# The experts of a routed mixture on one Trainium2 core: the last product of one expert set behind the first two of the next, and a spectrum computed in pieces between

## The chip, the cores and the metric

The kernel runs on one core of a Trainium2 chip. The metric is the device time of one launch in microseconds (us), the median of the runs; less is better. The engines named below are PE (matrix products), DVE (VectorE, elementwise), ACT (ScalarE), POOL (GpSimd, here indirect gathers and scatters) and SP (issues the large loads). Each runs its own instructions in a fixed order, and they wait for each other through semaphores.

## The reference, cut to what matters

Two transformer blocks run in a row. The first ends in a mixture of 32 experts, of which each of the 1024 tokens goes to two. The reference, cut to the part of an expert:

```python
def run(args):                                   # one block of tokens of one expert
    xblk, e = args
    hid = jax.nn.silu(xblk @ w1[e]) * (xblk @ w3[e])   # 1024 -> 512, twice
    return hid @ w2[e]                                 # 512 -> 1024

yb = lax.map(run, (xb, blk_expert)).reshape(cap, D) * buf_w[:, None]
y = jnp.zeros((N, D)).at[buf_tok].add(yb)        # back to the tokens
```

The second block needs, long before its first product, the spectrum of a filter: for each of 1024 channels an implicit filter (a small product times a decaying window), its absolute sum, and its transform by tables of cosines and sines. It depends on nothing that the experts compute, so the kernel works it out while the experts run.

## The kernel before

**The experts.** The kernel sorts the tokens to 32 experts and gives them places: place 0 to 11 are "large" (one slot of 128 tokens; places 1 to 3 have a second slot of 64 tokens), places 12 to 31 are "small" (64 tokens each; two small ones share one gather of 128 rows). They run as: place 0, then eleven large ones, and behind each of the first ten of these a pair of small ones. Ten times, therefore, the program goes through a group of three: large, small, small.

**One expert** is `block(w, slots)` (L1442). Its weights come in six pieces of 1 MB: four of `w1` and `w3`, two of `w2`. `weights` (L217) handles each piece: SP loads it into one of five `raw` tiles (L223), ACT rounds it to a high part `hi` (L228), DVE takes the difference `lo` (L230); there are three pairs of `hi` and `lo` tiles, and a pair is free again when PE has used it. The products are three matmuls per tile in this split arithmetic (L235 to L237), or two where 64 tokens' high and low parts stand side by side (L1459, L1460). Then

- `h` (two PSUM banks, tag `mm`; the second slot's have tag `acc`) holds x·w1 and x·w3. ACT and DVE make silu(h1)·h3 in the tile `hs` (L1465, L1466; for 64 tokens L1470 to L1473, where the halves are added first);
- PE transposes `hs` into PSUM (L1476), ACT and DVE split it into `sh` and `sl` (L1479, L1480);
- PE multiplies by `w2` into two banks of tag `acc` (with two slots, the first slot's into `mm`); DVE scales the result into `yo` (L1496), and POOL adds it to the tokens by an indirect DMA (L1497).

All of this is written expert by expert. Tokens come by `gather` (L1423): an indirect DMA into one of three `xg` tiles (L1428), PE transposes (L1435), and a split by ACT and DVE into `x` (two tiles, L1438, L1439).

**The spectrum** is a generator (L291) that is drained in one go behind the last of the 32 experts (L1534). It has PSUM banks of its own (`sp`, two) and one tile of most kinds; so the output tile `so` (L368, L369) is one tile, and two SP transfers of 256 KB each (L371) must have written it to DRAM before it can be filled again.

**What sets the order.** The program is not run in the order in which it is written: a scheduler takes the written order as a priority and lays each engine's instructions in a list at build time, moving later work into gaps that it expects. So pieces of the spectrum stand between the experts' matmuls in the kernel before, too, and a few matmuls of the next expert stand ahead of the transposes of one. The list of each engine is then fixed.

Of the kernel before, what the change touches and what calls it, by code (L numbers as in the profile page):

```python
# [15 lines left out]
P = 128  # L16
# [5 lines left out]
NTWO = 3  # L22
NLARGE = 12

C1 = NLARGE
# [93 lines left out]
class Builder:  # L119
# [171 lines left out]
    def spectrum(self, fp):  # L291
# [17 lines left out]
        for b in range(2):  # L309
# [14 lines left out]
            for q in range(8):  # L324
# [17 lines left out]
                if q == 0:  # L342
                    nc.vector.tensor_tensor(asum, ab, sd[q][1], op=ALU.max)
                else:
                    nc.vector.tensor_tensor(ab, ab, sd[q][1], op=ALU.max)
                    nc.gpsimd.tensor_tensor(asum, asum, ab, op=ALU.add)
            t = self.sp()
# [3 lines left out]
            for u in range(2):  # L351
                for mm in range(2):
# [9 lines left out]
                    nc.vector.tensor_add(ev[0], ev[0], q[1])  # L362
                    for n in range(2):
# [6 lines left out]
                        for v in range(2):  # L370
                            nc.sync.dma_start(spec[4 * b:4 * b + 4, :, 2 * u + v, mm + 2 * n, :].rearrange("c p n -> p c n"),  # L371
                                              o[:, v, :].rearrange("p (c n) -> p c n", n=P))

# [1033 lines left out]
    def moe(self):  # L1407
        nc, tc, I = self.nc, self.tc, self.i
        h2 = self.scr["h2"]
        with ExitStack() as cx:  # L1410
# [31 lines left out]
            def block(w, slots, eng=None):  # L1442
# [18 lines left out]
                hs = []  # L1461
                for n, (rows, x, tcol, gcol) in zip(N, slots):
# [4 lines left out]
                    else:  # L1467
# [5 lines left out]
                        nc.vector.tensor_mul(s[0:64], s[0:64], v[0:64])  # L1473
                    t = self.tp((P, 4, rows))
# [6 lines left out]
                    hs.append((sh, sl))  # L1481
# [23 lines left out]
            def place(b):  # L1505
                return of(nc.sync.value_load(self.order[0:1, b - 1:b], min_val=0, max_val=31))

            def large(b):
# [7 lines left out]
                return slots  # L1516

            def small(c):

                x = gather(self.tokI[:, c:c + 1], P, True)  # L1520
                for e, (t, g) in enumerate(((self.tokI[0:64, c:c + 1], self.gateS[0:64, c:c + 1]),
                                            (self.tokB[:, c - C1:c - C1 + 1], self.gateB[:, c - C1:c - C1 + 1]))):
                    block(place(NLARGE + 2 * (c - C1) + e), [(64, x[:, :, e], t, g)])

            block(lambda nm: I[nm][0, 0], large(0), nc.gpsimd)

            rest = list(range(NTWO + 1, NLARGE))
            for n, at in enumerate((2, 5, 8)):
                rest.insert(at, n + 1)
            for n, b in enumerate(rest):  # L1530
                block(place(b), large(b))
                if n < C2 - C1:
                    small(C1 + n)
# [5 lines left out]
            with tc.For_i(0, count, 1) as it:  # L1539
# [5 lines left out]
                block(of(reg), [(P, gather(tk), tk, gk)])  # L1545
# [390 lines left out]
```

## Time and profile before

| | |
|---|---|
| median of 3 runs | 3360.79 us (3357.3 to 3363.08) |
| the profiled execution | 3357.9 us, span 3356.1 us |
| busy share of the span | PE 92%, DVE 73%, ACT 39%, POOL 7% |
| experts, 1282 to 2075 us of the span | 793 us: PE busy 685.83, DVE 606.55, ACT 464.48 us |
| in that stretch | granted clock 0.93 of full, DMA share 0.81, 281 GB/s |

The span is that of one execution taken by the profiler; what lies around it (1.8 us) is the same for both kernels. Busy PE is a union of matmuls that overlap in their pipeline. [...] The DMA share is the mean busy share of the core's 16 DMA engines.

### The profile page before, as it was taken

The page shows a single profiled execution, that of the slowest core. Times are in us where ns is not written, and L with a number is a line of the kernel's source. Part 1 is how long each engine was busy: PE and PEld are TensorE (multiplying, and loading weights), DVE is VectorE, ACT ScalarE, POOL GpSimd, SP SyncE. Part 2 cuts the span into 40 slices and gives each one's busy share as a digit, 9 for nine tenths or more (in the row PEclk, how much of TensorE's full clock was granted, in tenths as well). Part 3 has the DMA queues.
Part 4 walks back from the last instruction along what each step waited for, and adds up shares of the span by engine and source line. Part 5 has one row for each costly group of instructions (what it writes and reads, how often), then busy time and mean ns, then how long its engine had stood idle before and what let it go on. Part 6 is the DMA issues. An engine that isn't in the chain of part 4 may idle for free. (4 is left out here: it accounts for less than half of the span.)

```text
span 3356.1 us, 41235 instructions
## 1 busy us (share of the span) xinstructions
PE 3077.4 (92%) x15219; PEld 2438.3 (73%) x15219; DVE 2438.7 (73%) x4447; ACT 1305.6 (39%) x1990; POOL 237.0 (7%) x143
## 2 busy tenths in 40 slices
PE   5999999999999959897899876899999999999998
PEld 4789999877777826565566554688887788888886
DVE  7888878667676577878778665577778765755767
ACT  3443333455543225657656554422233221221222
POOL 0000000000000012312213111000000000000000
PEclk9999999999999959998899988899999999999999
DMA  5653424244247346988789875322124311111111
GB/s 189 197 185 117 125 73 130 76 141 131 87 143 267 132 149 241 325 260 289 259 291 314 292 244 178 137 76 76 63 76 170 113 51 50 51 51 48 47 38 69
DMA packets 287912, 499.16 MB, mean 149 GB/s; under 512 B 21482, under 2 KB 176278, under 8 KB 286685
## 3 DMA queue, kind: packets, MB, share of 16 engines
q1 hardware_dynamic: 272925, 465.03, 40.8%
q0 software_dynamic: 6976, 16.79, 2.1%
q10 hardware_dynamic: 7808, 14.68, 1.2%
q8 instruction: 121, 1.98, 0.2%
q14 instruction: 82, 0.67, 0.1%
HBM read 431.92 MB, written 72.38 MB: 150 GB/s over the span
## 5 line engine op out<-in xcount | busy, mean ns | idle before, releaser
L230 DVE TENSOR_TENSOR lo<-raw,hi 128x2048 fp32r<-128x2048 f32 (+1 forms) x274 | 531.7, 1957 | 220.0 <-ACT hi L228 216.7
L228 ACT CAST hi<-raw 128x2048 fp32r<-128x2048 f32 (+1 forms) x276 | 449.6, 1644 | 270.3 <-PE acc L237 144.5
L243 PE MATMUL mm<-y_lo,hi 128*128 128x512 f32 x1072 | 423.1, 395 | 0.0
L244 PE MATMUL mm<-y_hi,lo 128*128 128x512 f32 x1072 | 423.0, 395 | 0.0
L246 PE MATMUL mm<-y_hi,hi 128*128 128x512 f32 x1072 | 273.6, 395 | 0.0
L243 PEld LDWEIGHTS mm<-y_lo,hi 128*128 128x128 f32 x1072 | 201.7, 188 | 44.9 <-DVE y_lo L215 0.2
L244 PEld LDWEIGHTS mm<-y_hi,lo 128*128 128x128 f32 x1072 | 201.7, 188 | 44.6
L246 PEld LDWEIGHTS mm<-y_hi,hi 128*128 128x128 f32 x1072 | 200.9, 188 | 44.5
L1852 DVE SCALAR_TENSOR_TENSOR cv<-gpad,fcw,cv 128x1024 f32<-128x1024 f32 x176 | 225.9, 1283 | 5.1
L243 PE MATMUL mm<-h_lo,hi 128*128 128x512 f32 x448 | 179.2, 401 | 0.5 <-DVE h_lo L215 0.5
L244 PE MATMUL mm<-h_hi,lo 128*128 128x512 f32 x448 | 178.0, 398 | 0.0
L416 DVE SCALAR_TENSOR_TENSOR ada<-araw,c,ada 128x512 f32<-128x512 f32 (+1 forms) x176 | 139.9, 795 | 30.9 <-DMA araw<-in_mod_w 15.8
L1459 PE MATMUL mm<-lo,x 128*128 128x512 f32 x320 | 137.5, 430 | 26.7 <-DVE lo L230 22.3
L243 PE MATMUL mm<-lo,h_hi 128*128 128x256 f32 x512 | 135.8, 296 | 0.1
L244 PE MATMUL mm<-hi,h_lo 128*128 128x256 f32 x512 | 133.3, 291 | 0.0
L1460 PE MATMUL mm<-hi,x 128*128 128x512 f32 x320 | 128.0, 400 | 0.0
L246 PE MATMUL mm<-h_hi,hi 128*128 128x512 f32 x448 | 121.8, 398 | 0.0
L1497 POOL DMA_INDIRECT d_x<-yo,tokI x25 | 96.5, 3859 | 345.4 <-DVE yo L1496 311.5
L235 PE MATMUL acc<-hi,sh 128*64 128x512 f32 (+1 forms) x256 | 117.2, 458 | 3.5 <-ACT sh L1479 3.5
L236 PE MATMUL acc<-lo,sh 128*64 128x512 f32 (+1 forms) x256 | 111.4, 435 | 0.0
L1796 ACT CAST hi<-raw 128x2048 fp32r<-128x2048 f32 (+2 forms) x36 | 63.6, 1767 | 122.7 <-PE tp L246 115.9
L1848 DVE TENSOR_SCALAR cv<-gpad,fcw,fcb 128x1024 f32<-128x1024 f32 x22 | 17.9, 814 | 121.7 <-ACT gpad L1842 121.6
(621 smaller groups left out, 6947.7 us busy)
## 6 DMA issues: line engine op xcount, KB each, us to landing
raw<-in_w SPq DMA_DIRECT2D x192, 1024.0 KB
araw<-in_mod_w SPq DMA_DIRECT2D x96, 256.0 KB
raw<-in_w_in SPq DMA_DIRECT2D x22, 1024.0 KB
raw<-in_ffn_w_up SPq DMA_DIRECT2D x44, 512.0 KB
araw<-in_w_ada SPq DMA_DIRECT2D x64, 256.0 KB
raw<-in_hy_w_in SPq DMA_DIRECT2D x12, 1024.0 KB
araw<-in_w_ada SPq DMA_DIRECT2D x16, 512.0 KB
d_G<-cy ACTq DMA_DIRECT2D x16, 512.0 KB
```

Source lines behind the costliest of these rows:

```text
L228: nc.scalar.copy(fh[:, qs], fr[:, qs])
L230: (eng or nc.vector).tensor_tensor(fl[:, qs], fr[:, qs], fh[:, qs].bitcast(F32), op=ALU.subtract)
L235: nc.tensor.matmul(out, lhs[0], rhs[0], start=start, stop=False)
L236: nc.tensor.matmul(out, lhs[0], rhs[1], start=False, stop=False)
L243: nc.tensor.matmul(out, a[0], b[1], start=start and k == 0, stop=False)
L244: nc.tensor.matmul(out, a[1], b[0], start=False, stop=False)
L246: nc.tensor.matmul(out, a[0], b[0], start=False, stop=stop and k == n - 1)
L416: V.scalar_tensor_tensor(acc, raw, c[:, k:k + 1], acc, op0=ALU.mult, op1=ALU.add)
L1459: nc.tensor.matmul(h[n][u], xx, wt[1][:, k, :], start=kk == 0, stop=False)
L1460: nc.tensor.matmul(h[n][u], xx, wt[0][:, k, :], start=False, stop=kk == 7)
L1497: nc.gpsimd.indirect_dma_start(out=self.x1, out_offset=bass.IndirectOffsetOnAxis(ap=tcol, axis=0), in_=yo[0:rows], in_offset=None, bounds_ ...
L1852: nc.vector.scalar_tensor_tensor(c3, g[:, di:di + 16, dj:dj + 64], col(k), c3, op0=ALU.mult, op1=ALU.add)
```

## The change

`block` is cut into three: `hidden` (products by w1 and w3, and `hs`), `turned` (transposes of `hs`, `sh` and `sl`) and `result` (product by w2 and the scatter). A loop takes the experts from a generator, one ahead: the gather of an expert is written ahead of the expert before it; then `hidden` of this expert, `result` of the one before it, `turned` of this one. The weights are loaded in the same changed order (four pieces of one expert, then the two pieces of w2 of the one before). The spectrum gets more `yield`s (40 pieces behind the loads at its start), and two pieces are written behind each of the 20 small experts. No product, no byte and no tile is added or removed.

```diff
@@ spectrum @@
                     nc.gpsimd.tensor_tensor(asum, asum, ab, op=ALU.add)
+                yield
...
                     nc.vector.tensor_add(ev[0], ev[0], q[1])
+                    yield
...
                             nc.sync.dma_start(spec[4 * b:4 * b + 4, :, 2 * u + v, mm + 2 * n, :].rearrange("c p n -> p c n"),
                                               o[:, v, :].rearrange("p (c n) -> p c n", n=P))
+                        yield
@@ moe @@
-            def block(w, slots, eng=None):
+            def hidden(w, slots, eng=None):
...
-                hs = []
+                out = []
...
+                    out.append(s)
+                return out
+
+            def turned(slots, hs):
+
+                out = []
+                for (rows, x, tcol, gcol), s in zip(slots, hs):
                     t = self.tp((P, 4, rows))
...
-                    hs.append((sh, sl))
+                    out.append((sh, sl))
+                return out
+
+            def result(w, slots, hs):
+
+                N = range(len(slots))
...
-            block(lambda nm: I[nm][0, 0], large(0), nc.gpsimd)
-
-            rest = list(range(NTWO + 1, NLARGE))
-            for n, at in enumerate((2, 5, 8)):
-                rest.insert(at, n + 1)
-            for n, b in enumerate(rest):
-                block(place(b), large(b))
-                if n < C2 - C1:
-                    small(C1 + n)
...
+            def experts():
+
+                yield from large(0)
+                rest = list(range(NTWO + 1, NLARGE))
+                for n, at in enumerate((2, 5, 8)):
+                    rest.insert(at, n + 1)
+                for n, b in enumerate(rest):
+                    yield from large(b)
+                    if n < C2 - C1:
+                        yield from small(C1 + n)
+
+
+            todo, before = experts(), None
+            nxt = next(todo)
+            while nxt:
+                (b, slots), nxt = nxt, next(todo, None)
+                w = place(b)
+                hs = hidden(w, slots, None if b else nc.gpsimd)
+                if before:
+                    result(*before)
+                before = w, slots, turned(slots, hs)
+
+                for _ in range(2 if b >= NLARGE else 0):
+                    next(spectrum, None)
+            result(*before)
             for _ in spectrum:
                 pass
```

Three places of the engines' lists show what this does. Line numbers of the kernel after are larger by 3 in `gather` and `hidden`, by 10 in `turned`, by 11 to 15 in `result`.

**PE at the end of a small expert.** Before, the four transposes of `hs` stand behind the last hidden matmuls (`mm<-..,x`) of the same expert, with one matmul of the spectrum (`sp`) between, and the w2 products (`acc<-..,sh`) behind them:

```order
L1459 MATMUL mm<-lo,x 128x512
L1460 MATMUL mm<-hi,x 128x512
L366 MATMUL sp<-sd_17807,dftl 128x512
L1476 MATMUL tp<-ident,hs 128x64 x4
L1435 MATMUL tp<-ident,xg_12745 128x128 x3
L235 MATMUL acc<-hi,sh 64x512
L236 MATMUL acc<-lo,sh 64x512
```

After, in the same place, the transposes stand behind the 24 w2 products of the expert before, and hidden matmuls of the next expert follow:

```order
L235 MATMUL acc<-hi,sh 128x512
L236 MATMUL acc<-lo,sh 128x512
L237 MATMUL acc<-hi,sl 128x512
L1486 MATMUL tp<-ident,hs 128x64 x4
L368 MATMUL sp<-sd_13872,dftl 128x512
L368 MATMUL sp<-sd_13887,dftl 128x512
L1438 MATMUL tp<-ident,xg_12744 128x128 x4
L1462 MATMUL mm<-lo,x 128x512
L1463 MATMUL mm<-hi,x 128x512
```

Between the matmuls that fill `h` and the transposes of `hs` there now stand 24 matmuls that need neither.

**DVE near the end of the spectrum.** `so` (L370, L371 after the change) is one tile, and `lo` is the splitting of a weight piece. After, two fillings of `so` stand this close:

```order
L370 TENSOR_TENSOR so<-ev,sp 128x512
L371 TENSOR_TENSOR so<-sp,ev 128x512
L230 TENSOR_TENSOR lo<-raw,hi 128x2048 x2
L370 TENSOR_TENSOR so<-ev,sp 128x512
L371 TENSOR_TENSOR so<-sp,ev 128x512
L230 TENSOR_TENSOR lo<-raw,hi 128x2048 x2
L1469 TENSOR_TENSOR hs<-hs,mm 128x512
```

In the kernel before, one of the closest two fillings has this between them, on the same engine:

```order
L368 TENSOR_TENSOR so<-ev,sp 128x512
L1439 TENSOR_TENSOR x<-tp,x 128x8x64 x2
L230 TENSOR_TENSOR lo<-raw,hi 128x2048
L369 TENSOR_TENSOR so<-sp,ev 128x512
L230 TENSOR_TENSOR lo<-raw,hi 128x2048
L1471 TENSOR_TENSOR hs<-mm,hs 64x512
L230 TENSOR_TENSOR lo<-raw,hi 128x2048
L368 TENSOR_TENSOR so<-ev,sp 128x512
```

There, two pieces of `lo` and a short instruction lie between a filling's end and the next one's start. Of the sixteen fillings three have come closer to the one before them than any is before: with two pieces of `lo` between (the one shown), with two and a scaled result, and with one piece and five short instructions. The spectrum also ends later: before, a third of the experts' rows in PE's list stand behind its last matmul; after, under a twentieth.

**PE and DVE at an expert with two slots** (three of the 32). After, PE's products by w2 of the expert before stand right behind the hidden matmuls of the second slot, and both write banks of tag `acc`:

```order
L1462 MATMUL acc<-lo,x 128x512
L1463 MATMUL acc<-hi,x 128x512
L235 MATMUL acc<-hi,sh 64x512
L236 MATMUL acc<-lo,sh 64x512
L237 MATMUL acc<-hi,sl 64x512
```

So they wait until DVE has read these banks out; on DVE the second of those two reads (`hs<-acc`, L1474) now stands here:

```order
L1474 TENSOR_TENSOR hs<-acc,hs 64x512
L230 TENSOR_TENSOR lo<-raw,hi 128x2048
L1442 TENSOR_TENSOR x<-tp,x 128x8x64 x2
L1469 TENSOR_TENSOR hs<-hs,mm 128x512
L1474 TENSOR_TENSOR hs<-acc,hs 64x512
```

One piece of `lo`, two splits of `x` and a product have come to stand between the two reads.

## Rows read from the trace of the kernel before

**Rows 1.** The page: engines' busy time, and slices of the span.

```profile
PE 3077.4 (92%) x15219; PEld 2438.3 (73%) x15219; DVE 2438.7 (73%) x4447; ACT 1305.6 (39%) x1990; POOL 237.0 (7%) x143
...
PEclk9999999999999959998899988899999999999999
...
GB/s 189 197 185 117 125 73 130 76 141 131 87 143 267 132 149 241 325 260 289 259 291 314 292 244 178 137 76 76 63 76 170 113 51 50 51 51 48 47 38 69
```

**Rows 2.** Stretches: start:end, length; busy PE, PEld, DVE, ACT, POOL; PEclk, DMA share, GB/s.

```profile
0.00:1199.00 1199.00, 1113.32 (x6754) 943.98 (x6754) 885.99 (x2575) 484.54 (x1080) 37.68 (x62) 0.99 0.44 142
1282.00:2075.00 793.00, 685.83 (x2666) 461.41 (x2664) 606.55 (x501) 464.48 (x389) 168.46 (x62) 0.93 0.81 281
2092.00:3356.10 1264.10, 1219.32 (x5655) 1001.87 (x5655) 874.93 (x1204) 334.38 (x496) 2.18 (x2) 0.98 0.23 75
```

**Rows 3.** The same view over three of the ten groups: the first two and the last.

```profile
1305.90:1376.80 70.90, 65.89 (x252) 42.78 (x252) 57.18 (x47) 41.46 (x34) 18.35 (x5) 0.95 0.91 320
1376.80:1453.30 76.50, 67.39 (x266) 45.94 (x265) 57.44 (x49) 42.19 (x37) 15.41 (x7) 0.93 0.94 319
...
1997.00:2070.00 73.00, 56.27 (x213) 39.78 (x213) 51.83 (x39) 40.72 (x32) 10.60 (x3) 0.86 0.68 241
```

**Rows 4.** Waits, 1282 to 2075 us: who waited for whom, us, times, longest.

```profile
DVE lo L230 <- ACT hi L228: 167.6, 54, 6.1
ACT hi L228 <- PE acc L237: 144.5, 55, 6.3
PE tp L1476 <- DVE hs L1473: 56.6, 15, 6.6
PE mm L1459 <- DVE lo L230: 22.3, 15, 5.9
DVE hs L1471 <- ACT hs L1470: 5.5, 11, 1.1
PE tp L1476 <- DVE hs L1466: 4.2, 3, 2.6
```

**Rows 5.** Timeline of a small expert: start, us, instruction, idle before and releaser.

```profile
2026.45 0.66 PE L1476 MATMUL tp<-ident,hs 64*128 64x64 f32 x4 [4.43 <-DVE hs L1473]
2027.57 0.69 PE L235 MATMUL acc<-hi,sh 128*64 128x512 f32 x1 [0.46 <-ACT sh L1479]
...
2032.32 0.47 PE L237 MATMUL acc<-hi,sl 128*64 128x512 f32 x1
2032.63 0.39 PE L235 MATMUL acc<-hi,sh 128*64 128x512 f32 x1
2032.86 0.39 PE L236 MATMUL acc<-lo,sh 128*64 128x512 f32 x1
...
2040.67 0.50 PE L1459 MATMUL mm<-lo,x 128*128 128x512 f32 x1 [1.38 <-DVE lo L230]
...
2044.61 0.40 PE L1460 MATMUL mm<-hi,x 128*128 128x512 f32 x1
...
2049.28 0.52 PE L1476 MATMUL tp<-ident,hs 64*128 64x64 f32 x4 [4.28 <-DVE hs L1473]
```

**Rows 6.** Groups by line, 1282 to 2075 us: count, busy us, mean ns, idle before.

```profile
L230 DVE TENSOR_TENSOR lo<-raw,hi 128x2048 fp32r<-128x2048 f32 x188 | 425.3, 2283 | 168.1 <-ACT hi L228 167.6
L228 ACT CAST hi<-raw 128x2048 fp32r<-128x2048 f32 x187 | 354.3, 1906 | 211.7 <-PE acc L237 144.5 <-issue 26.9 <-PE acc L1460 16.2
...
L1439 DVE TENSOR_TENSOR x<-tp,x 128x512 fp32r<-128x512 f32 (+1 forms) x48 | 30.1, 645 | 1.7 <-ACT x L1438 1.7
...
L1471 DVE TENSOR_TENSOR hs<-mm,hs 64x512 f32<-64x512 f32 x40 | 27.1, 678 | 3.1 <-ACT hs L1470 2.4
L1476 PE MATMUL tp<-ident,hs 64*128 64x64 f32 (+1 forms) x136 | 20.4, 284 | 60.8 <-DVE hs L1473 56.6 <-DVE hs L1466 4.2
```

**Rows 7.** Timeline of DVE: two fillings of so, neither preceded by a wait.

```profile
1481.20 0.68 DVE L369 TENSOR_TENSOR so<-sp,ev 128x512 f32<-128x512 f32 x1
...
1489.38 0.68 DVE L368 TENSOR_TENSOR so<-ev,sp 128x512 f32<-128x512 f32 x1
```

More of the change, by code (lines that the diff above doesn't have):

```diff
@@ L1505, in place @@
             def place(b):
-                return of(nc.sync.value_load(self.order[0:1, b - 1:b], min_val=0, max_val=31))
+                return of(nc.sync.value_load(self.order[0:1, b - 1:b], min_val=0, max_val=31)) if b else lambda nm: I[nm][0, 0]
             def large(b):
@@ L1515, in large @@
                     slots.append((64, gather(t, 64, True)[:, :, 0], t, g))
-                return slots
+                yield b, slots
             def small(c):
                 x = gather(self.tokI[:, c:c + 1], P, True)
-                for e, (t, g) in enumerate(((self.tokI[0:64, c:c + 1], self.gateS[0:64, c:c + 1]),
-                                            (self.tokB[:, c - C1:c - C1 + 1], self.gateB[:, c - C1:c - C1 + 1]))):
-                    block(place(NLARGE + 2 * (c - C1) + e), [(64, x[:, :, e], t, g)])
-            block(lambda nm: I[nm][0, 0], large(0), nc.gpsimd)
-            rest = list(range(NTWO + 1, NLARGE))
-            for n, at in enumerate((2, 5, 8)):
-                rest.insert(at, n + 1)
-            for n, b in enumerate(rest):
-                block(place(b), large(b))
-                if n < C2 - C1:
-                    small(C1 + n)
+                yield NLARGE + 2 * (c - C1), [(64, x[:, :, 0], self.tokI[0:64, c:c + 1], self.gateS[0:64, c:c + 1])]
+                yield NLARGE + 2 * (c - C1) + 1, [(64, x[:, :, 1], self.tokB[:, c - C1:c - C1 + 1], self.gateB[:, c - C1:c - C1 + 1])]
+            def experts():
[19 more added lines that the diff above has]
+            result(*before)
             for _ in spectrum:
@@ L1544, in moe @@
                 reg = nc.sync.value_load(self.eob[0:1, bass.ds(it, 1)], min_val=0, max_val=31)
-                block(of(reg), [(P, gather(tk), tk, gk)])
+                w, slots = of(reg), [(P, gather(tk), tk, gk)]
+                result(w, slots, turned(slots, hidden(w, slots)))
         self.psum(mm=4, acc=2, tp=2, aux=0)
```

## The prediction

> **What bounds the kernel now.** Read the page first: PE is busy 92% of the span, but the granted clock falls under 0.9 in a short dip (slice 14, counted from 0) and again in slices 18, 19 and 23 to 25, and in slices 16 to 23 the transfer rate is highest [rows 1]. That piece, slices 15 to 24, is the experts. Cut the span into stretches [rows 2]: ahead of the experts and behind them PE is busy 93% and 96% of the time at a clock of 0.99 and 0.98. In the 793 us of the experts PE is busy 685.83 us at 0.93, DVE 606.55 us, and the DMA engines 0.81 of the time. Nothing is full there, so something takes turns.
>
> The waits say what [rows 4]. Of the 107 us in which PE idles (793 - 686), 60.8 are spent in front of the transposes of `hs` [rows 6], until DVE has made it (56.6 and 4.2). Another 22.3 us go to pieces of `lo`. The conversions in turn wait for PE: ACT 144.5 us until a `w2` product frees a `hi` tile, DVE 167.6 us for ACT. One small expert shows the order of events [rows 5]: PE idles 4.43 us, transposes, starts the `w2` products at 2027.57, and for 4.75 us (to 2032.32) issues one matmul every 0.43 us; from 2032.63 on one every 0.23 us. [...] The next expert's hidden products wait once more, 1.38 us, and at 2045 PE stops again for 4.28 us. The period is 22.8 us, of which 4.3 is the wait and about 2.2 the lower clock.
>
> **What the change removes.** With 24 `w2` products of the expert before standing between hidden products and transposes, PE has 24 x 0.23 = 5.5 us of work in the 4.3 us that silu takes. I count the wait at nothing then: 60.8 us. The cover is these products, and they need the w2 pieces in time; if those are late, PE waits for `lo` in the same place.
>
> The clock: 11 matmuls at 0.43 instead of 0.23 cost 2.2 us [rows 5], and PE's own waits for `hs` number 18 [rows 4]. If each brings one such stretch, 18 x 2.2 = 40 us. It is an estimate; the bounds are 0 and 58 us (a mean clock of 0.93 over 793 us means half speed in 111 us, and if PE were busy in all of it, half would be saved).
>
> So PE alone would need 793 - 61 - 40 = 692 us.
>
> **What is late next.** Everything else in the stretch is still to be done in the shorter time. DVE has 606.55 us of it; in 692 that is 88%. The transfers have 0.81 x 793 = 642 busy us of the DMA engines; in 692 that would be 93%. Groups of three experts exist that already run at 0.91 and 0.94 [rows 3]: they took 70.9 and 76.5 us, and they hold much of the spectrum's traffic. The last group, which has none, runs at 0.68 and yet takes 73.0 us, so it is bound by turns, not by bytes. The change spreads the spectrum over nearly all groups, so every group comes to look like the first, without its waits. I take 0.91 as the share that can be held on average: 642 / 0.91 = **706 us**. At 0.94 it would be 683, below PE's 692. So transfers set the end, and 793 - 706 = 87 us is the gain ahead of what the change adds.
>
> [...]
>
> The chain through the three weight pairs must also hold. A piece costs ACT 1.91 and DVE 2.28 us [rows 6]. PE frees a pair; 4.2 us later at best it is full again; meanwhile PE has two other pieces, 2 x 8 x 0.23 = 3.7 us for a small expert's hidden products, 5.5 for all others. So in the small experts a wait of 0.5 us or so per piece remains, like the 1.38 us of [rows 5] but shorter. Four such pieces in 20 experts make at most 40 us of PE's time, and PE's chain has only 14 us to spare under the 706: this is why I don't take more.
>
> **What the change adds.**
> - Two-slot experts, three of them. PE's `w2` products of the expert before need banks that DVE must first read out, and on DVE a piece of `lo` (2.28), two splits of `x` (2 x 0.65) and a product (0.68, like L1471's) stand ahead of the second read (0.68) [rows 6]: 4.9 us. Lowest is nothing, if DVE is ahead of PE there. Highest is 4.9 with a stretch of lower clock, 7.1 each. I take 5, because nothing else is ready on PE's list: +15 us (0 to 21).
> - `so`, a single tile. Three fillings come closer to the one before. No row before shows a wait for its two writes; the shortest distance seen is from 1481.88 to 1489.38, 7.5 us, without a wait [rows 7]. So the writes take 7.5 us or less there. The new distances in DVE's work are 4.6, 5.1 and 6.5 us, so at most 2.9 + 2.4 + 1.0 = 6 us are waited; if the writes land sooner, nothing. I take 3.
> - Gathers one expert ahead: the instructions are the same, POOL is busy 168.46 of 793 us [rows 2], and its waiting costs nobody; scatters may stand behind a gather. Nothing. The spectrum's pieces: same instructions, already in the busy times above; nothing, as long as DMA is the bound, for it is their cover too.
>
> Sum: 793 - 87 + 15 + 3 = 724 us, a gain of 69 us. From the profiled 3357.9 us that makes 3289; the median of the runs lies 2.9 above that execution, so **3292 us** (2.0% less). Its own range, from shares of 0.87 to 0.94: 3265 to 3324.
>
> **The rivals.**
> - PE's chain sets the end. Transfers reach 0.94 in the second group [rows 3] while PE was waiting, so perhaps more without it; no extra waits. 692 us, a gain of 101: 3260 us. Against it: the average would have to be what the best group shows. 0.17.
> - Half of it. PE waits less at `hs` but more at `lo`, one or two waits of 1.4 us per expert beyond what was there, since three pairs must now feed PE without a pause. 692 + 1.5 x 1.4 x 32 = 759, a gain of 34: 3327 us. For it: 22.3 us of such waits exist already, and 167.6 us of DVE's waiting for ACT [rows 4] show that the pairs are short. 0.20.
> - The change does nothing: the pieces arrive no faster than now, and what was waited at `hs` is waited elsewhere, with no gain and no loss: 3361 us. Against it stands the last group's 0.68. 0.04.
> - Slower: DVE's fixed order. The read-outs of `h` (L1474) stand in DVE's list ahead of pieces of `lo` that PE wants next, and wait for ACT, which waits for PE's last hidden matmul. If the piece behind them comes 4.3 us late, PE stops at `lo` as it did at `hs`, at the lower clock behind it, so the 101 us come back and the 18 us added stay, with about 6 more at `so`: 3361 + 24 = 3385 us. It decides from 69 / 32 = 2.2 us of new waiting per expert. Against it: DVE waited only 5.5 us in all for these copies [rows 4], and the read-outs' neighbours in its list are nearly the same as before. 0.09. [...]
>
> **How the numbers follow.** Forecast 0.50, the others 0.17, 0.20, 0.04 and 0.09. A measurement of this kernel tells about 0.2% (7 us) from no change. The range from 3250 to 3340 us holds the first three cases but for their tails and leaves out the last two: 0.8. Faster by over 0.2%: 0.87; within 0.2%: 0.04; slower: 0.09.
>
> **What would show it.** PE's waits at the transposes of `hs` under 10 us, the granted clock of the stretch at 0.97 or more, a DMA share near 0.9, and the stretch of the experts near 724 us; PE's remaining waits at `lo`, and three of about 5 us at matmuls into `acc` behind two-slot experts. Before and behind the experts nothing moves. I am wrong if the clock stays at 0.93 (waits have only moved), or if DVE shows waits of several us at `so`, or if the DMA share stays near 0.81 while the time falls less than 30 us.

## The result, and the profile after

The changed kernel takes 3248.48 us (median of 4 runs, 3248.01 to 3251.59), the kernel before 3359.05 us (4 runs, 3351.78 to 3363.08): a ratio of 0.9675, 95% interval 0.9657 to 0.9693, so 109 us (103 to 115) less. The prediction said 3292 us, 69 less, with a range from 3250 to 3340. The direction was right; the gain is half as large again as forecast, and the time lies 1.5 us under the range.

The page after: busy time of the engines, PE's granted clock in 40 slices (a share of full), and the transfer rate (against [rows 1]).

```profile
PE 3045.8 (94%) x15219; PEld 2422.8 (75%) x15219; DVE 2442.4 (75%) x4447; ACT 1303.0 (40%) x1988; POOL 243.6 (8%) x143
...
PEclk9999999999999976999999998999999999999999
...
GB/s 194 192 186 130 87 123 80 123 132 141 91 121 230 197 127 143 366 339 344 326 305 292 312 336 154 100 72 78 57 143 183 49 42 52 52 39 52 46 40 72
```

The clock stays in its highest tenth through all the slices of the experts (16 to 23), where before it fell in slices 18, 19 and 23, and the transfers run at 292 to 366 GB/s there. The same stretches as in [rows 2], after (length; busy PE, PEld, DVE, ACT, POOL; clock, DMA share, GB/s):

```profile
0.00:1199.00 1199.00, 1112.77 (x6754) 943.78 (x6754) 887.58 (x2589) 484.54 (x1082) 37.61 (x62) 0.99 0.44 143
1282.00:1966.00 684.00, 652.23 (x2671) 444.15 (x2669) 608.50 (x500) 462.49 (x387) 173.25 (x61) 0.99 0.92 325
```

Ahead of the experts nothing has moved. What stands behind them takes 1263.7 us after (1983.0 to 3246.7) and 1264.1 before. The experts themselves take 684 us instead of 793. Their work is the same: DVE 608.50 and ACT 462.49 us busy, and 325 GB/s x 684 us = 222 MB, as before. PE's busy time fell by 33.6 us (685.83 to 652.23), with the clock at 0.99 instead of 0.93, and its idle time by 75.4 (107.2 to 31.8): together 109 us.

Groups of about three experts, the same view (against [rows 3]): four early ones, the slowest two and the last.

```profile
1349.80:1410.00 60.20, 58.79 (x252) 41.41 (x252) 53.87 (x44) 40.30 (x32) 16.07 (x7) 1.00 0.99 359
1410.00:1475.00 65.00, 62.70 (x271) 43.52 (x270) 60.84 (x51) 44.37 (x39) 17.70 (x6) 1.00 0.96 342
1475.00:1537.90 62.90, 59.88 (x244) 40.24 (x243) 56.06 (x47) 41.60 (x34) 18.47 (x5) 1.00 0.96 335
1537.90:1610.00 72.10, 68.90 (x273) 45.24 (x272) 56.59 (x48) 45.06 (x38) 18.08 (x6) 1.00 0.94 345
1610.00:1684.60 74.60, 70.21 (x281) 46.73 (x280) 70.29 (x63) 53.87 (x51) 16.89 (x9) 0.98 0.84 296
1684.60:1756.90 72.30, 61.49 (x235) 39.83 (x234) 64.07 (x55) 52.67 (x45) 29.95 (x9) 0.93 0.83 292
...
1893.50:1954.40 60.90, 60.24 (x243) 40.64 (x242) 54.96 (x44) 40.09 (x32) 13.38 (x3) 1.00 0.93 323
```

A share of 0.94 was the best of the three groups shown before. After, four groups in a row hold 0.94 to 0.99, and the last one 0.93 instead of 0.68. Next to that stand PE at 0.95 or more of most groups and DVE at 0.78 to 0.94: nobody has much room left. The waits in the stretch (who for whom, us, times, longest; against [rows 4]):

```profile
DVE lo L230 <- ACT hi L228: 42.6, 29, 5.8
ACT hi L228 <- PE mm L237: 27.4, 18, 6.0
ACT hi L228 <- PE mm L1463: 24.8, 16, 5.1
ACT hi L228 <- DMA raw<-in_w: 24.5, 18, 6.9
ACT hi L228 <- PE acc L237: 24.3, 16, 3.6
PE mm L1462 <- DVE lo L230: 9.9, 10, 2.4
PE acc L236 <- DVE lo L230: 7.3, 12, 1.2
PE sp L350 <- POOL asum L346: 5.1, 1, 5.1
DVE so L370 <- DMA d_spec<-so: 0.7, 1, 0.7
```

The waits of PE at the transposes of `hs` are gone. ACT no longer waits 144.5 us for `w2` products before it can fill a `hi` tile, but in four kinds of 24 to 27 us, one of them the load of the raw piece. PE's timeline at the end of an expert, where 4.43 us were waited in [rows 5]:

```profile
1896.12 0.39 PE L235 MATMUL acc<-hi,sh 128*64 128x512 f32 x1
1896.35 0.39 PE L236 MATMUL acc<-lo,sh 128*64 128x512 f32 x1
...
1901.40 0.39 PE L237 MATMUL acc<-hi,sl 128*64 128x512 f32 x1
1901.63 0.60 PE L1486 MATMUL tp<-ident,hs 128*128 128x128 f32 x4
1901.98 0.48 PE L1462 MATMUL mm<-lo,x 128*128 128x512 f32 x1
```

The 24 `w2` products of the expert before (a small one) run from 1896.12, one every 0.23 us, for 5.5 us, and the transposes (of a large one) start behind them without an idle gap. That is the mechanism of the prediction, with the 5.5 us that it worked out.

### The profile page after: what moved, and what is told of

Read it like the earlier page. It is cut to its first block, busy times and chain, and to the rows that moved or that the text cites. A ratio compares the mean times of both kernels' runs of the same rounds, so it can differ in the third digit from the quotient of the medians.

```text
span 3246.7 us, 41208 instructions
## 1 busy us (share of the span) xinstructions
PE 3045.8 (94%) x15219; PEld 2422.8 (75%) x15219; DVE 2442.4 (75%) x4447; ACT 1303.0 (40%) x1988; POOL 243.6 (8%) x143
## 5 line engine op out<-in xcount | busy, mean ns | idle before, releaser
L1462 PE MATMUL mm<-lo,x 128*128 128x512 f32 x320 | 139.7, 436 | 10.1 <-DVE lo L230 9.9
L236 PE MATMUL acc<-lo,sh 128*64 128x512 f32 (+1 forms) x256 | 107.2, 419 | 7.3 <-DVE lo L230 7.3
L243 PEld LDWEIGHTS mm<-h_lo,hi 128*128 128x128 f32 x448 | 84.3, 188 | 23.6 <-ACT cpad L649 2.6
L237 PE MATMUL acc<-hi,sl 128*64 128x512 f32 (+1 forms) x256 | 101.9, 399 | 0.0
```

The costliest lines, as they stand in the source:

```text
L236: nc.tensor.matmul(out, lhs[0], rhs[1], start=False, stop=False)
L237: nc.tensor.matmul(out, lhs[1], rhs[0], start=False, stop=stop)
L243: nc.tensor.matmul(out, a[0], b[1], start=start and k == 0, stop=False)
L1462: nc.tensor.matmul(h[n][u], xx, wt[1][:, k, :], start=kk == 0, stop=False)
```

## The experiments

The change has three parts: the order of the products, the gathers one ahead, and the spectrum's pieces between. Five runs take them apart, five more cut the work of one, two or three resources to find what holds the experts at 684 us, and the rest try the clock by itself and other ways on. Ratios are to the kernel before, run beside them; in microseconds they are taken of 3360. "Experts" is the stretch from 1282 us to the same place of each kernel's end of the experts; in e1_order and e15_order_alone the spectrum ends well behind the experts, so their stretches stand in the text.

| run | median us | ratio, 95% interval | experts us | PE busy, DVE busy | clock | DMA share |
|---|---|---|---|---|---|---|
| after | 3248.5 | 0.9675 (0.9657 to 0.9693) | 684 | 652, 609 | 0.99 | 0.92 |
| e15_order_alone | 3280.9 | 0.9760 (0.9745 to 0.9775) | see text | | | |
| e1_order | 3273.7 | 0.9734 (0.9714 to 0.9754) | see text | | | |
| e4_gather_late | 3265.6 | 0.9700 (0.9677 to 0.9723) | 698 | 667, 611 | 0.97 | 0.91 |
| e3_gather_ahead | 3347.7 | 0.9953 (0.9938 to 0.9969) | 778 | 685, 610 | 0.93 | 0.83 |
| e2_pieces | 3367.5 | 1.0008 (0.9996 to 1.0020) | 801 | 696, 608 | 0.93 | 0.81 |
| e5_fewer_bytes | 3232.9 | 0.9616 (0.9600 to 0.9632) | 667 | 645, 611 | 0.99 | 0.73 |
| e6_less_pe | 3249.2 | 0.9659 (0.9641 to 0.9678) | 685 | 613, 607 | 0.97 | 0.93 |
| e7_both | 3223.8 | 0.9593 (0.9577 to 0.9610) | 655 | 602, 607 | 0.98 | 0.74 |
| e10_less_dve | 3225.1 | 0.9579 (0.9559 to 0.9599) | 660 | 604, 472 | 0.97 | 0.94 |
| e11_three | 3153.4 | 0.9372 (0.9355 to 0.9388) | 590 | 581, 468 | 0.99 | 0.80 |
| e8_before_dummies | 3354.8 | 0.9976 (0.9964 to 0.9987) | 796 | 766, 612 | 0.98 | 0.81 |
| e13_clock | 3346.2 | 0.9951 (0.9936 to 0.9966) | 778 | 737, 607 | 0.98 | 0.83 |
| e9_pairs | 3306.3 | 0.9828 (0.9807 to 0.9848) | 738 | 672, 613 | 0.98 | 0.88 |
| e16_raws | 3270.0 | 0.9727 (0.9714 to 0.9740) | 703 | 660, 609 | 0.96 | 0.89 |
| e12_pool | 3315.0 | 0.9851 (0.9834 to 0.9869) | 738 | 667, 612 | 0.96 | 0.86 |
| e14_spread | 3250.5 | 0.9657 (0.9640 to 0.9674) | 684 | 654, 608 | 0.99 | 0.92 |

### The three parts of the change

**The order and the gathers, without the pieces between.** Of after:

```
-                for _ in range(2 if b >= NLARGE else 0):
-                    next(spectrum, None)
```

> The changed order of the experts and the gathers one ahead, without the spectrum's pieces written between (the spectrum is drained behind the last expert, as before). Theory A (the gain of 111 us is the order: no waits at `hs`, 61 us, and no low clock behind them, 34 to 40 us, plus about 10 us of waits for `x`): 3245 to 3265 us, no wait at the transposes of `hs`, clock 0.98 or more. Theory B (the pieces written between matter too, because they even out the load of the transfers and give PE work where a weight piece is late): 3275 us or more, with waits for `lo` in groups of experts that hold much of the spectrum. My prediction counted the pieces at nothing, so it goes with A.

Measured: 3273.74 us, 0.9734. That lies between the two theories, close to B, and the trace says B: no wait at `hs`, a clock of 1.00, and yet 20 us behind after. The stretches of this run:

```profile
1282.00:1885.00 603.00, 569.51 (x2487) 405.68 (x2487) 560.62 (x430) 434.47 (x353) 144.59 (x54) 1.00 0.97 350
...
1900.00:1950.00 50.00, 42.94 (x68) 15.52 (x69) 26.43 (x37) 13.08 (x17) 4.31 (x4) 0.70 0.47 137
1950.00:1990.00 40.00, 35.42 (x72) 15.27 (x72) 15.50 (x24) 4.87 (x8) 4.52 (x4) 0.78 0.27 81
```

The experts are done by about 1890 us, at a share of 0.97. But much of the spectrum is still to do, alone, until about 2008 us, and up to 1990 at a clock of 0.70 to 0.78 and a share of 0.47 and less. Up to 1961 us the chain that ends last goes round between POOL's sum `asum`, ACT and DVE, one turn in 3.5 us; behind that it goes from PE to DVE to the transfer of `so` and back:

```profile
1979.87 3.45 PE sp L368 x8
1983.34 0.69 DVE so L370
...
1984.65 2.60 DMA d_spec<-so
1987.37 0.69 DVE so L370
...
1988.71 1.98 PE sp L359 x4
1990.69 3.45 PE sp L368 x8
```

The second of these chains cannot overlap itself, since `so` is one tile. With the pieces written between the experts all this lies under their work.

**The pieces alone.** Of after, with the order of before and the gather behind the result:

```
-                if before:
-                    result(*before)
-                before = w, slots, turned(slots, hs)
+                result(w, slots, turned(slots, hs))
```

> The order of before (w2's products and the transposes of an expert right behind its own hidden products, its gather not ahead), with two pieces of the spectrum written behind each small expert. Theory A: the waits at the transposes of `hs` stay (about 61 us) and so does the lower clock: 3345 to 3365 us, nothing gained. Theory B: pieces of the spectrum fall into the waits and fill a part of them: 3300 to 3335 us.

Measured: 3367.52 us, 1.0008. Theory A. The waits at the transposes stay (56.8 and 6.8 us). In the kernel before, the build had found gaps for the spectrum by itself: its last product by the tables started at 1820.6 us, long before the end of the experts at 2075. So the pieces gain nothing in the old order and 20 us in the new one, where no gaps are left that pull the spectrum forward.

**The gathers ahead alone.** The order and the spectrum of before, only `nxt` taken one ahead.

> Only the gathers one expert ahead; order of the products and the spectrum as before. The trace of before has 10 us of PE's waits at products and transposes for `x`, and the trace of after has none. If they are worth their time by themselves: 3345 to 3352 us. My prediction's step (nothing, since other waits hide them): 3355 to 3363 us. In both the waits at `hs` stay near 60 us.

Measured: 3347.69 us, 0.9953 (16 us less; 10 to 21). My step "nothing" was wrong. PE's waits at `x` are gone, which in the kernel before were these:

```profile
PE mm L235 <- ACT x L1438: 6.0, 4, 1.9
PE mm L1459 <- DVE x L1439: 4.0, 1, 4.0
```

Those at `hs` are 18.0 instead of 60.8 us; but those at `lo` (34.0 and 8.2) and at `hi` (25.1) have grown, so most of it only moved. The expectation that `hs` stays near 60 was wrong too: the build lays the lists differently when the gather is there earlier. At 2035.78 us of this trace, for example, the first hidden matmul of a large expert stands ahead of the transposes of `hs` of the small one before it, and PE waits there, for `hi`.

**The gathers late, the rest as after.**

```
-                (b, slots), nxt = nxt, next(todo, None)
+                b, slots = nxt
...
                 for _ in range(2 if b >= NLARGE else 0):
                     next(spectrum, None)
+                nxt = next(todo, None)
```

> After, but the gather of an expert is written behind the previous one's result instead of ahead of its hidden products; everything else as in after. If the gather ahead is worth something only once PE's list has no other gaps: 3256 to 3275 us, with PE waiting for `x` or its transposes again (10 us or more, and the clock lower behind them). If it is worth nothing, as predicted: 3245 to 3253 us.

Measured: 3265.56 us, 0.9700. PE waits again at `x` and at its transposes (8.0, 4.5, 3.8 and 2.7 us), as the first theory said. But 0.9700 (0.9677 to 0.9723) and after's 0.9675 (0.9657 to 0.9693) overlap, so of the 8 us only the sign is likely.

**The order alone.**

> The changed order of the experts alone: no gather ahead, no pieces between (the spectrum behind the last expert). By the runs with two of the three parts, if their prices add up (gather 8 to 16 us, pieces 20 us): 3275 to 3290 us. If the order needs the gather ahead, because x must now be there while PE has no other gap: 3295 us or more.

Measured: 3280.87 us, 0.9760, 81 us less (76 to 86). The last expert's result is scaled at 1956.0 us, and the spectrum's last product by the tables starts at 2015.1. PE has no wait at `hs` to speak of (0.6 us), but waits for `x` (18.8, 11.5 and 1.9 us). The parts add up: the order 81, the pieces 20 (from 0.9760 to 0.9700 without the gather ahead, from 0.9734 to 0.9675 with it; the intervals of each couple are apart), the gathers 8 to 9 (intervals overlap).

### What holds the experts at 684 us

**A third fewer weight bytes.** Of after, in `hidden`; `weights` converts the last raw piece again where it is given none, so w3's products are computed from w1:

```
-self.weights(src, 2, 1024, eng if kg == 0 else None, True)
+self.weights(None if u else src, 2, 1024, eng if kg == 0 else None, True)
```

> After, but the pieces of w3 are not loaded: w1's raw piece is converted once more in their place (the result differs). A third fewer weight bytes; conversions, matmuls and order are as in after. Theory T (transfers set the end of the experts now, as my prediction's 706 us said, only at a share of 0.92 to 0.99 instead of 0.91): the 684 us fall by 50 us or more, to about PE's busy time; total 3190 us or less. Theory P (PE's own work at full clock sets it, 652 us busy in 684; rival of the prediction): at most the 32 us of PE's idle time can go, and those only where a piece is late; total 3225 to 3248 us, with the DMA share near 0.65.

Measured: 0.9616, 20 us less than after.

```profile
1282.00:1949.00 667.00, 645.45 (x2672) 444.64 (x2670) 610.66 (x501) 462.83 (x387) 173.22 (x61) 0.99 0.73 236
```

The share falls to 0.73 and the stretch only by 17 us. Theory T, which wanted 50, falls: with room in the transfers the experts still take 667 us. The total, 3232.9, is in the span of theory P; the next run tests that one.

**A third less work in w2's products.**

```
-self.mm3(y[n][u][0:rows], (sh[:, kk, :], sl[:, kk, :]), (wt[0][:, k, us], wt[1][:, k, us]), kk == 0, kk == 3)
+nc.tensor.matmul(y[n][u][0:rows], sh[:, kk, :], wt[0][:, k, us], start=kk == 0, stop=False)
+nc.tensor.matmul(y[n][u][0:rows], sh[:, kk, :], wt[1][:, k, us], start=False, stop=kk == 3)
```

> After, without the third product (high part of the weights with the low part of `hs`) in w2's products, so the result is coarser: 8 of 24 matmuls per slot less, some 35 slots of 8 x 0.23 = 1.84 us, about 65 us of PE's work; transfers and conversions are as in after. Theory P: 3185 to 3205 us (45 to 65 us less). Theory T: 3235 to 3250 us, with PE waiting for `hi` or `lo` instead and the DMA share at 0.92 or more.

Measured: 0.9659; after's interval covers it.

```profile
1282.00:1967.00 685.00, 612.65 (x2419) 409.91 (x2418) 606.78 (x498) 467.64 (x391) 188.03 (x61) 0.97 0.93 325
```

PE has 40 us less to do and the stretch ends in the same place: it waits instead, 27.8, 12.4 and 11.0 us for `lo` and 10.1 for `hi`. So theory P falls as well, although PE was busy 95% of the stretch. By itself this run looks like theory T, as the one before looked like P; only the two together rule both out. The clock is 0.97 here instead of 0.99, and PE's busy time fell by 40 us (652.23 to 612.65), where 0.23 us a matmul had given an estimate of 65.

**Both cuts.**

> Both edits together (w3's pieces not loaded, the third product of w2's left out). If PE and the transfers each hold the other's gain back, this gains more than the two alone together: 3150 us or less. If P holds, it gives what the run with less PE work gives, plus at most the waits for late pieces: 3170 to 3200 us. If DVE (608 us busy in the 684) is next, the stretch cannot fall under some 625 us: 3185 us or more.

Measured: 0.9593, 28 us less than after: about the sum of the two (20 and 5). Neither had hidden the other's gain. DVE, 607 us busy of 655, was next in the expectation.

**Less for DVE.** Of after, without w2's low part: `lo` is not made (64 pieces), and its product is left out instead of the third one, so PE has the same matmuls as in e6.

```
-        for qs in parts:
+        for qs in parts if low else ():
             (eng or nc.vector).tensor_tensor(fl[:, qs], fr[:, qs], fh[:, qs].bitcast(F32), op=ALU.subtract)
...
+nc.tensor.matmul(y[n][u][0:rows], sl[:, kk, :], wt[0][:, k, us], start=False, stop=kk == 3)
```

> After, without the low part of w2: its `lo` is not made and the product with it is left out, so the result is coarser. PE has the same matmuls less as in the run with less PE work (which stayed at 685 us for the experts), and DVE has 64 x 2.28 = 146 us less; transfers as in after. Theory D (DVE, 608 us busy in the 684, and the turns around it set the end together with the transfers): 635 to 665 us for the experts, total 3200 to 3230 us, with the DMA share at 0.96 or more. Theory T alone (transfers at 0.92 can't go faster): 675 us or more, total 3240 us or more.

Measured: 0.9579, 27 us less than e6, with as many matmuls and bytes. Two things differ from e6: DVE has less work, and a `w2` piece is ready after ACT's 1.91 us, without DVE's 2.28, so that it comes to PE sooner. The run can't tell the two apart, nor does any run take DVE's work away without a third of the `w2` products.

```profile
1282.00:1942.00 660.00, 603.89 (x2399) 408.73 (x2398) 471.70 (x434) 460.28 (x386) 172.42 (x60) 0.97 0.94 337
```

It is in the span of theory D, with a share of 0.94, a little under the 0.96 that D wanted. PE still waits 32.3 and 11.9 us for `lo`, of w1 and w3.

**All three cuts.**

> The run with both cuts (w3's pieces not loaded, a third of w2's products left out) and DVE's 146 us less as well. Theory D: the 655 us of the run with both cuts fall to 600 to 625 us, where PE (602 us busy) is the end; total 3170 to 3195 us. If the ring of three pairs holds and not DVE's load: 640 us or more, total 3208 us or more.

Measured: 0.9372, 74 us less than e7 and 102 less than after; the total lies 17 us below the lower end of theory D's.

```profile
1282.00:1872.00 590.00, 580.83 (x2402) 405.08 (x2401) 468.04 (x434) 462.22 (x389) 197.22 (x60) 0.99 0.80 267
```

PE is busy in 581 of 590 us: now it is PE that sets the end, and the ring of three pairs does not stop it (for `hi` it is as in after; of the `lo` tiles the `w2` pieces use none here). With a third of the `w2` products left out throughout, DVE's 146 us are worth 27 us while all bytes are loaded (e6 to e10), and 74 us with a third fewer (e7 to e11); a third of the weight bytes is worth 22 us with all of DVE's work (e6 to e7), and 70 without its 146 us (e10 to e11). So at 684 us transfers and `lo` on DVE hold the end together. PE's work by itself is worth 5 us there, which the intervals do not tell from nothing.

### The clock by itself

**Idle matmuls in the kernel before.**

```
+                y = None
+                if len(slots) == 1:
+                    y = [[self.acc() for _ in range(2)]]
...
+                    for _ in range(16):
+                        nc.tensor.matmul(D2, D0, D1, start=True, stop=True)
```

(D0 and D1 are parts of the expert's `x`, D2 is the bank.)

> Before, plus 16 idle matmuls (the expert's own `x` times itself, into a bank that w2's products then overwrite) written behind the hidden products of each expert with one slot, so that PE is not idle while `hs` is made; order and waits otherwise as in before. It separates the two parts of the gain. If the clock falls because PE idles there, and costs the 40 us that my prediction took (0 to 58): clock of the stretch 0.98 or more and 3320 to 3345 us, since 16 x 0.23 = 3.7 us fit into the wait of about 4.3 us. If the clock costs nothing on the path: 3355 to 3365 us in spite of a clock of 0.98. If the idle matmuls are in the way (they can't start at once, or last longer than the wait): over 3370 us.

Measured: 0.9976, 8 us less, with a clock of 0.98. The run says little of the price, since the build laid the idle matmuls among the hidden products: in PE's timeline nine of sixteen stand ahead of the last `w3` piece's products, seven at most behind, and PE then still waits for `hs`.

```profile
2039.28 2.22 PE L1470 MATMUL acc<-x 128*128 128x512 f32 x9
...
2043.20 0.39 PE L1470 MATMUL acc<-x 128*128 128x512 f32 x1
...
2045.29 1.54 PE L1470 MATMUL acc<-x 128*128 128x512 f32 x6
2051.56 0.68 PE L1486 MATMUL tp<-ident,hs 64*128 64x64 f32 x4 [4.73 <-DVE hs L1483]
```

**Idle matmuls that need the last `lo` piece**, so that they can only run in the wait:

```
+                    for _ in range(12):
+                        nc.tensor.matmul(y[0][0], wt[1][:, 3, 0:P], wt[1][:, 3, :], start=True, stop=True)
```

> Before, plus 12 idle matmuls behind the last `lo` piece of the hidden products of each expert with one slot (that piece by itself, into a bank that w2's products then overwrite), so that they can only run in the wait for `hs`: 12 x 0.23 = 2.8 us of the 4.3 us. Order, loads and conversions as in before; one pair of `hi` and `lo` is held up to 2.8 us longer. If the lower clock behind the waits was worth what the prediction priced (40 us, 0 to 58): clock 0.98 or more and 3315 to 3340 us. If PE's own work gets shorter by some 30 us but the loop of pairs (ACT and DVE refill what w2's products free) sets the pace: clock 0.98 and 3345 to 3362 us. If holding the pair longer matters: over 3365 us.

Measured: 0.9951, 16 us less (11 to 22): 3346 us, the second of the three cases.

```profile
1282.00:2060.00 778.00, 736.82 (x3013) 512.11 (x3011) 606.69 (x502) 465.49 (x389) 175.70 (x62) 0.98 0.83 286
```

With the clock at 0.98, PE's own work takes an estimated 737 - 348 x 0.23 = 657 us, 29 less than before, close to the 33.6 that after gained. But the time falls by only about half of that. So in the old order the lower clock cost some 29 us of PE's time and some 16 us of the end. Waits that are there anyway take up the rest (DVE still waits 139.2 us for ACT, and PE 25.6 at `hs`). The run also holds a pair of tiles longer, and what that takes off the gain is not priced.

### Other ways on

**Four pairs and three raw tiles**, in the memory of three and five: `self.wpool(cx, "We", 3, 4, side="right")`.

> After, with four pairs of `hi` and `lo` tiles instead of three, and three `raw` tiles instead of five (the same memory). Theory R (the ring of three pairs ties PE, ACT and DVE to each other, and so costs what no single engine's load shows): 3215 to 3238 us, ACT's waits for PE's matmuls (some 95 us before `hi` in after) go down. Theory T (transfers): three `raw` tiles leave fewer loads under way, so 3255 us or more. Neither: 3244 to 3252 us.

Measured: 0.9828, 51 us slower than after: theory T. The waits in the stretch show it; in after this one was 24.5 us:

```profile
ACT hi L228 <- DMA raw<-in_w: 178.2, 107, 6.3
```

ACT's waits for PE nearly vanish (5.7 and 2.4 us are the largest), but as two things were changed the run cannot price the fourth pair by itself.

**Six raw tiles**, for one gather tile and one `yo` tile less.

> After, with six `raw` tiles instead of five, paid with one gather tile less (two) and one `yo` tile instead of two. Computes the same. If the number of loads under way holds the transfers back: 3230 to 3245 us. If the transfers are at their rate with five, and DVE holds the rest: 3246 to 3252 us. If the single `yo` (DVE waits for its scatter) or the two gather tiles are in the way: 3253 us or more, with DVE's or PE's waits there.

Measured: 0.9727, 17 us slower than after, by the price that was paid: DVE waits 25.3 us for the scatter of `yo`, three times up to 12.6, and PE 17.5 us at the transposes of `x`. What a sixth tile is worth stays open.

**`lo` of the second w2 piece on POOL.**

```
-2, 1024, None, True)
+2, 1024, nc.gpsimd if kg else None, True)
```

> After, with the `lo` of the second w2 piece of each expert on POOL instead of DVE: 32 x 2.28 = 73 us less for DVE, 32 x 4.78 = 153 us more for POOL (173 us busy of 684 in after). Computes the same as after. Theory D: 3210 to 3238 us. Theory R (the turn of a piece through the three pairs counts, not DVE's load): a piece takes 2.5 us longer on POOL, so 3250 to 3280 us, with new waits at w2's products for POOL's `lo`.

Measured: 0.9851, 59 us slower than after. PE waits 44.7 us for POOL's `lo`, as theory R said, though the total is far above its 3250 to 3280. But the run did not relieve DVE either, and so is no test of D: DVE has 32 pieces less and is busy 612 us, longer than in after. Its groups by line show why (count | busy us, mean ns | idle before):

```profile
L230 DVE TENSOR_TENSOR lo<-raw,hi 128x2048 fp32r<-128x2048 f32 x156 | 393.1, 2539 | 51.5 <-ACT hi L228 51.4
L1476 DVE TENSOR_TENSOR hs<-hs 64x512 f32<-64x512 f32 x23 | 51.8, 2252 | 3.6 <-ACT hs L1475 2.8
L1474 DVE TENSOR_TENSOR hs<-mm,hs 64x512 f32<-64x512 f32 x40 | 27.2, 679 | 9.8 <-ACT hs L1473 9.5
```

**One piece of the spectrum behind each large expert too.**

```
-                for _ in range(2 if b >= NLARGE else 0):
+                for _ in range(2 if b >= NLARGE else 1):
```

> After, with one piece of the spectrum written behind each large expert too (two behind each small one, as in after). Computes the same. If evenness of the load is what the pieces are worth: 3235 to 3246 us, with the low DMA share and clock of the two groups 1610 to 1757 us of after (0.84 and 0.83) nearer to the others. If the place doesn't matter as long as the pieces end before the experts do: 3246 to 3251 us. If the spectrum's tables then crowd the weights early, where the share is 0.96 to 0.99 already: 3252 to 3270 us.

Measured: 3250.48 us, 0.9657: no difference from after that can be told. The group with the low share has only moved forward: 1610.0 to 1684.6 now has 0.76, and 1684.6 to 1756.9 has 0.95. So in these two runs the place of the pieces doesn't matter, as long as they end before the experts do. No run that keeps all of the products and bytes is faster than after by more than its interval.

## Why the prediction came out as it did

- **The wait at `hs`, 60.8 us:** right. The trace after has no wait there, under the cover that was named.
- **The clock, 40 us (0 to 58):** nearly right as PE's time: 33.6 us less busy at 0.99. At the expert of [rows 5] the view of before has the clock at 0.50 while a matmul starts every 0.43 us, and at 1.00 while one starts every 0.23:

```profile
2027.57:2032.30 4.73, 4.73 (x11) 2.52 (x12) 1.27 (x2) 0.00 (x0) 0.00 (x0) 0.50 1.02 406
...
2032.63:2038.00 5.37, 5.37 (x25) 3.69 (x24) 3.18 (x3) 4.27 (x3) 0.00 (x0) 1.00 0.28 115
```

  (The bound of 58, from half speed in 111 us, is 56 by its own figures.) As time of the end in the old order e13 shows some 16 us. In after the wait went with it, and PE's busy and idle time together fell by the whole 109 us.
- **PE alone, 692 us:** PE needed 652 us and idled 31.8, together 684. The 8 us less are 15 us more of idle time gone than forecast (75.4 instead of 60.8; 10 of them are the waits at `x`) and, against them, a smaller gain of the clock (33.6 instead of 40).
- **"I take 0.91 as the share that can be held on average ... So transfers set the end", 706 us:** this is the step that failed. The value came from two groups of before, in which PE waited and did not ask for more; taken as what the transfers can hold, it was only what they were asked. After, the mean is 0.92, four groups hold 0.94 to 0.99, and e1_order holds 0.97 over 603 us. And transfers don't set the end by themselves: e5 takes 29% of the bytes away (236 GB/s x 667 us = 157 MB) and gains 17 us. They do it with DVE's `lo`; DVE's 88% the prediction had worked out and then passed over. The term should have been 684 instead of 706, which is 22 us of the error: 14 from taking the transfers' 706 over PE's 692, and the 8 above. The forecast's own range came from the same share, and its lower end, 3265, does not come out: 0.94 gives 683, PE's 692 would then set the end, and that makes 3278. Nor do the traces show a rate at which the transfers stop: after moves 359 GB/s over 60 us, e1_order 382 over 82 us (last section).
- **Two-slot experts, +15 us (0 to 21):** nothing, the other 15 us of the error's main part. The prediction let PE wait for both read-outs of `h`; but in PE's list the `w2` products fill the first bank with 12 matmuls before they need the second. PE's and then DVE's timeline at one of the three:

```profile
1416.42 0.40 PE L235 MATMUL acc<-hi,sh 128*64 128x512 f32 x1
...
1418.95 0.40 PE L237 MATMUL acc<-hi,sl 128*64 128x512 f32 x1
1419.18 0.38 PE L1486 MATMUL tp<-ident,hs 128*128 128x128 f32 x2
1419.32 0.47 PE L235 MATMUL acc<-hi,sh 128*64 128x512 f32 x1
...
1418.40 0.68 DVE L1474 TENSOR_TENSOR hs<-acc,hs 64x512 f32<-64x512 f32 x1
1419.38 0.74 DVE L1511 SCALAR_TENSOR_TENSOR yo<-acc,gateB,g2row 64x512 f32<-64x512 f32 x1 [0.30 <-PE acc L237]
```

  The second read-out ends at 1419.08, and the matmul that needs its bank starts at 1419.32, 0.37 instead of 0.23 us behind the twelfth, since two transposes stand between. That the first bank is full behind the twelfth shows on DVE, which scales it from 1419.38 on. The list of PE's waits in the stretch has none at these banks, at any of the three. The cover of 12 x 0.23 = 2.8 us was overlooked; at the one shown it suffices by 0.24 us.
- **`so`, +3 us (0 to 6):** 0.7 us of waits. Right in kind.
- **Gathers ahead, nothing:** 8 to 16 us. The waits for `x` stood in the trace and were left out of the sum.
- **The pieces, nothing:** 20 us in the new order. The busy times were right; but the sum took for granted that the spectrum lies under the experts, and e1 and e15 show that without the pieces the new order pushes much of it out behind them.
- **The rivals.** "PE's chain sets the end" (692 us, 3260) came nearest in number, but its mechanism is not shown: e6 took work from PE and gained nothing. "Half of it" and "slower" feared new waits at `lo`: PE's are 20.6 us in all (9.9, 7.3 and the 3.4 at w1's and w3's products of full slots), against 22.3 before.

The sum, then: 724 - 684 = 40 us, of which 22 are the step with the share (with PE's 8), 15 the banks and 2 `so`. Of the prediction's own signs the clock, the end of the waits at `hs` and those left at `lo` came; the stretch near 724 us and the three waits at `acc` did not. That the order alone gives 81 us and the forecast of the whole was 69 shows the same from the other side: what was counted against the order did not come, and two parts counted at nothing brought 28.

## What to carry to other kernels

A share of busy transfers read off a stretch in which others wait is what was asked of them, not what they can do (0.91 and 0.94 in two groups of before, 0.97 over 603 us in e1_order): take a bound only from a stretch that is full, or forecast the range between it and full. Where three resources stand near 90% each, cut them one by one and then together: here PE's cut alone gave 5 us, that of the bytes alone 20, DVE's on top of PE's another 27, and all three together 102. And work that lies in gaps has to be given a place of its own when the gaps are closed.

## What was not expected of the hardware

In e12 DVE's operations that read SBUF alone took longer beside a long operation on POOL. The product `hs<-hs` (L1476, two operands in SBUF) took 2252 ns on average, and at most 5022, instead of 677 in after, and pieces of `lo` 2539 instead of 2310; the operation of the same size that reads PSUM (`hs<-mm,hs`, L1474) stayed at 679 ns (678 in after). In DVE's timeline of that run one such product starts at 1385.03 us and lasts 4.59; POOL's `lo` runs from 1384.55 for 4.52 us and ends 0.55 us before it. The same holds for the four others that start beside a `lo` of POOL between 1320 and 1480 us: each ends 0.55 or 0.56 us behind it.

```profile
1382.70 0.68 DVE L1474 TENSOR_TENSOR hs<-mm,hs 64x512 f32<-64x512 f32 x1 [0.36 <-ACT hs L1473]
1385.03 4.59 DVE L1476 TENSOR_TENSOR hs<-hs 64x512 f32<-64x512 f32 x1 [1.65 <-ACT hs L1475]
```

That is the price here: a product that takes 0.68 us in after ended, where it started beside a POOL operation of 4.5 us, only 0.55 us after that one. What holds DVE up there, no run shows.

The DMA engines held a share of 0.99 at 359 GB/s over 60 us while PE was busy 98% of the time, and 0.97 at 350 GB/s over 603 us in e1. Over 82 us of these the rate was higher still:

```profile
1470.00:1552.00 82.00, 74.46 (x324) 52.24 (x323) 78.26 (x56) 61.82 (x49) 20.99 (x7) 1.00 1.02 382
```

(The share of 1.02 stands so in the view; read it as full.) So at a full share the rate is not one fixed number in this kernel. PE's matmuls started every 0.23 us in the group at 359 GB/s, as they do at 115 GB/s in before (2032.63 to 2038.00 us, at the same clock of 1.00), so no contention between the two is to be seen.
